# GLA stage of a hybrid encoder: keys, inner tiles and v in split float32r, gated outputs transposed from float32r copies

## The chip, the cores and the metric

The kernel runs on one core of one Trainium2 chip. The metric is the device time of one execution in microseconds. The profile is one execution on the chip, recorded by the hardware profiler; PE is the matrix engine, PEld its weight loads, DVE the vector engine, ACT the scalar engine, POOL the GpSimd engine and SP the engine whose queue issues most loads. A queue's name ends in q (ACTq, SPq).

## What is computed

The reference is an encoder of two layers over 512 tokens of width 1024, all in float32. Layer 0 mixes tokens with bidirectional gated linear attention (GLA), layer 1 with softmax attention, and each is followed by a gated MLP with a width-3 convolution. Only the GLA mixer of layer 0 is touched. It has 4 heads with 128 key and 256 value columns each:

```python
def gla_chunked(q, k, v, log_a, strict):          # per head; one call forward, one on flipped inputs
    b = jnp.cumsum(log_a, axis=3)                  # within chunks of 64 tokens
    q_dec, k_inv = q * jnp.exp(b), k * jnp.exp(-b)
    att = jnp.where(mask, q_dec @ k_inv.T, 0.0)    # inner products of a chunk
    o_intra = att @ v
    kv_chunk = (k * jnp.exp(b_end - b)).T @ v      # what a chunk adds to the state
    ...                                            # state[n+1] = decay_chunk * state[n] + kv_chunk
    o_inter = q_dec @ s_prev
    return o_intra + o_inter

o = o_f + o_b
o = rmsnorm(o, norm_w) * jax.nn.silu(g)
return o @ w_out
```

## The kernel before

The kernel keeps the residual x as eight tiles of 128 features x 512 tokens (x[c]). Weights stream in over SP's queue into two raw buffers; the class Weights turns each half of 128x1024 into a high part in float32r (ACT copy, L220) and a low part (DVE subtract, L221). A product of two such split operands is three float32r matmuls: high x high, high x low, low x high (mm3, L385). A matmul on plain float32 tiles shows in the trace as two matmul records. L86 is the helper that issues nearly all matmuls, so they are told apart by the tile that they write.

Instructions are traced in the order of the program, and a scheduler at compile time then fixes each engine's queue: by the written order as priority, with what is ready by its own timing going first. So an engine's order can differ from the written one, but on the chip each engine follows its fixed queue. Tiles come from pools by tag with a number of buffers each: in SBUF "g" (22 buffers of 128x1024), "xhl" (8), and in the stage "t" (6) and "u" (4) of 128x512; in PSUM "acc" (3 banks), "s" (2), "pt" (2) and "po" (1).

The GLA stage, function gla (L462):

- Four segments (seg, L474) project the normalised input to v and g, in token layout: 4 PSUM banks per segment, one for each block of 128 tokens, 512 columns (two heads) wide. seg_out (L481) evicts each bank with one DVE instruction that scales by the norm (L485). v and g are four tiles each, one per token block, holding all heads. Beside the segments run eight gates (gate, L532; two directions x 4 heads): a PE product z, then Abs, Exp and Ln on ACT, a POOL subtract (L544), a DVE scan, and two Exp that make EK (L563, L564).
- proj(h) (L581) makes k and q of head h, 24 float32r matmuls each. After proj(0), SiLU of g runs on ACT (L688) and POOL multiplies by the norm weights (L689), tile by tile.
- The loop over heads (L691) writes proj(h+1) and then core(h). core first multiplies EK by k and q (DVE, L597, L598) and makes "end" on POOL (L601). Then come the key transposes kt (three per direction, L608) and their copy to kts (ACT, L610); the inner products in (4 token blocks x 2 directions, float32, L620), put together in the tile at by an ACT copy (L622) and a predicated DVE copy (L625); per direction three products kv of kts and v (float32, L643) and their state updates (ACT L644, DVE L646). The third product of each direction goes to the one "po" bank. Then comes tail(h-1). Last, the outputs o (L667): per token block at with v, and EK with the states of one or both directions, all float32; then squares on ACT (L671), the inverse root (DVE L319, POOL L321) and the gating into g (DVE, L674).
- tail(h) (L676) transposes the two 128-column chunks of head h's gated output on PE (float32, L680) and splits them into oT (ACT L682, DVE L683), which lies in buffers of tag "xhl"; these come free as proj(3) finishes with the normalised input.
- The output projection op (out_steps, L426) runs twelve steps (chunks 0 to 5 for two pairs of output tiles), then tail(3), then the rest.

Of the kernel before, what the change touches and what calls it, by code (L numbers as in the profile page):

```python
# [59 lines left out]
def hybrid_encoder_kernel(  # L60
# [47 lines left out]
    def big(dt, n):  # L108
        return pair("g", 22, dt, n)
# [352 lines left out]
    def gla(norm, nxt):  # L462
# [5 lines left out]
        gc = big(F32, "gconst")  # L468
        mfull = gc[:, 0 : S + 1]
        gnw = gc[:, 640 : 640 + DV]  # L470
        v = [big(F32, "v") for _ in range(NT)]
        g = [big(F32, "g") for _ in range(NT)]

        def seg(i, between=None):  # L474
            ps = [bank(tag, "vg") for tag in SEG_BANKS[i]]
# [4 lines left out]

        def seg_out(ps, dst, h):  # L481
            for j in range(NT):
                o = dst[j][:, h * S : (h + 1) * S]
                r = norm.rtok[:, j : j + 1]
                dve.tensor_scalar(o, ps[j], r, None, ALU.mult)  # L485


        ps = seg(0)
# [100 lines left out]
            dve.scalar_tensor_tensor(kqt[:, :S], psq, DK ** -0.5, norm.R, ALU.mult, ALU.mult)  # L589
            return kqt  # L590

        def core(h, kqt, then):
            ends = big(F32, "end")
            ends = [ends[:, :S], ends[:, S:]]
            for d in range(2):
                e, f = EK[h, d], ends[d]
                dve.tensor_tensor(e[:, S:], e[:, S:], kqt[:, S:], ALU.mult)  # L597
                dve.tensor_tensor(e[:, :S], e[:, :S], kqt[:, :S], ALU.mult)  # L598
# [5 lines left out]
            orders, keys = ([0, 1, 2], [3, 2, 1]), []  # L604
            for d, order in enumerate(orders):
                kt = bank("pt", "kt")
                for i, s in enumerate(order):
                    pe.transpose(kt[:, i * P : (i + 1) * P], ends[d][:, s * P : (s + 1) * P], ident)  # L608
# [4 lines left out]
            at = tmp("t", "at")  # L613
            banks = []
            for d in range(2):
                e = EK[h, d]
                b = bank("acc" if h == GH - 1 else "s", "in")
# [6 lines left out]
            def upper():  # L624
                dve.copy_predicated(at3, msk, banks[1].rearrange("p (s c) -> p s c", c=P))  # L625

            at3 = at.rearrange("p (s c) -> p s c", c=P)
            msk = smask.rearrange("p (o c) -> p o c", o=1).to_broadcast([P, NT, P])

            st = {}  # L630
            hs = slice(h * DV, (h + 1) * DV)
            for d, order in enumerate(orders):
                kts = keys[d]
                sa = tmp("t", "sa")
                sb = tmp("t", "sb") if d == 0 else st["b"]
                st["b"] = sb
                step = 1 if d == 0 else -1
                kv = bank("acc", "kv")
                kv2 = bank("po", "kv2")
                place = [kv[:, :DV], kv[:, DV:], kv2[:, :DV]]  # L640
                slot = [sa[:, :DV], sa[:, DV:], sb[:, d * DV : (d + 1) * DV]]
                for i, s in enumerate(order):
                    mm(place[i], kts[:, i * P : (i + 1) * P], v[s][:, hs], start=True, stop=True)  # L643
                act.activation(slot[0], place[0], AF.Copy)  # L644
                for i in (1, 2):
                    last = dve.scalar_tensor_tensor(slot[i], slot[i - 1], FK[h, d][:, order[i] : order[i] + 1],  # L646
                                                    place[i], ALU.mult, ALU.add)
                for i, s in enumerate(order):
                    st[d, s + step] = slot[i]
                if d == 0:  # L650
                    with tc.issue_after(last.ins) if h == GH - 1 else ExitStack():
                        upper()
            if then is not None:
                then()

            oss = tiny(4, "oss")
            og = []
            for s in range(NT):
                if s % 2 == 0:
# [3 lines left out]
                for d in range(2):  # L663
                    if (d, s) in st:
                        parts.append((EK[h, d][:, s * P : (s + 1) * P], st[d, s]))
                for i, (l, r) in enumerate(parts):
                    mm(po, l, r, start=i == 0, stop=i == len(parts) - 1)  # L667
                og.append(po)
            for s in range(NT):
                junk = tmp("sq", "junk", DV)  # L670
                act.activation(junk, og[s], AF.Square, accum_out=oss[:, s : s + 1])  # L671
            ors = rsqrt_eps(oss, NT, "ors", 1.0 / DV)
            for s in range(NT):
                dve.scalar_tensor_tensor(g[s][:, hs], og[s], ors[:, s : s + 1], g[s][:, hs], ALU.mult, ALU.mult)  # L674

        def tail(h):  # L676
            for c in (2 * h, 2 * h + 1):
                tp = bank("pt", "tp")
                for s in range(NT):
                    pe.transpose(tp[:, s * P : (s + 1) * P], g[s][:, c * P : (c + 1) * P], ident)  # L680
                t = pair("xhl", 8, F32R, "oT")
                act.activation(t[:, :S], tp, AF.Copy)  # L682
                dve.tensor_tensor(t[:, S:], tp, t[:, :S].bitcast(F32), ALU.subtract)  # L683
                oh[c] = (t[:, :S], t[:, S:])

        kqt = proj(0)
        for j in range(NT):
            act.activation(g[j], g[j], AF.Silu)  # L688
            pool.tensor_tensor(g[j].rearrange("p (h c) -> p h c", c=DV), g[j].rearrange("p (h c) -> p h c", c=DV),  # L689
                               gnw.rearrange("p (o c) -> p o c", o=1).to_broadcast([P, GH, DV]), ALU.mult)  # L690
# [545 lines left out]
```

## Time and profile before

| what | value |
|---|---|
| median of 3 runs | 1117.07 us (1115.98 to 1118.34) |
| the profiled execution's own time | 1119.08 us |
| its span, first to last instruction | 1117.4 us |
| mean granted TensorE clock | 0.998 |
| GLA stage: segments and gates | about 5 to 104 us |
| GLA stage: heads, from k(0) to the end of o(3) | about 104 to 188 us |
| output projection | about 188 to 233 us |

The MLP of layer 0 follows until about 600 us, attention until about 745, the MLP of layer 1 to the end. In a row of a timeline stand the start in us, the duration, the engine, the line, the operation, out<-in with their tiles, the shape and a count; in brackets the idle time of the engine before it and what ended that. The chain of waits has the start, the duration and what the chain ran over. Matmul durations in the timeline overlap, since matmuls are pipelined; the chain's steps do not overlap, so that its duration over its count is the time one matmul takes from the next.

### The profile page before, as it was taken

Reading aid. Unit: us, or ns where it says so; the run is one execution under the profiler, and the core shown is the slowest. Engines: PE = TensorE matmul, PEld = TensorE weight load, DVE = VectorE, ACT = ScalarE, POOL = GpSimd, SP = SyncE. Lnnn points to the kernel's source line nnn. Section 1 sums busy time; section 2 is a strip of 40 time slices with the busy share of each in tenths; the row PEclk is TensorE's granted clock in tenths of the full one; section 3 lists DMA queues with packets and bytes.
Section 4 is the critical chain, followed back from the end, with each engine's and each line's share of the span. In section 5 each row is a group of like instructions: output and inputs, shape, how many; then the busy total and the mean of one; then the engine's idle time right before and its main releaser. Section 6 shows DMA issues by size and latency. Waiting matters only on the chain.

```text
span 1117.4 us, 16142 instructions
## 1 busy us (share of the span) xinstructions
PE 1104.9 (99%) x6418; PEld 974.1 (87%) x6418; DVE 864.3 (77%) x1325; ACT 601.0 (54%) x892; POOL 105.9 (9%) x96
## 2 busy tenths in 40 slices
PE   9999999999999999999999999999999999999998
PEld 7878888888899999999978887788879999999997
DVE  6566655459989999979885567654998999997985
ACT  6455224367645455544464788845764545544541
POOL 0213310021000000000004332101100000000000
PEclk9999999999999999999999999999999999999999
DMA  6323211368332322323337754446863232332322
GB/s 219 128 78 111 76 40 37 113 140 198 135 113 95 113 92 98 115 74 114 136 76 200 180 164 117 152 127 145 191 173 114 96 113 81 109 114 76 114 76 76
DMA packets 30938, 131.78 MB, mean 118 GB/s; under 512 B 3600, under 2 KB 4240, under 8 KB 22160
## 3 DMA queue, kind: packets, MB, share of 16 engines
q1 hardware_dynamic: 20496, 102.30, 27.5%
q0 software_dynamic: 5472, 19.93, 9.2%
q10 hardware_dynamic: 4896, 8.54, 2.1%
q8 instruction: 50, 0.82, 0.3%
q14 instruction: 24, 0.20, 0.1%
HBM read 100.34 MB, written 2.10 MB: 92 GB/s over the span
## 4 chain that ended last, share of the span: by engine, by line
PE 91%; DMA 3%; DVE 3%; ACT 2%; issue 1%; POOL 0%; SPq 0%; DVEq 0%; POOLq 0%; ACTq 0%
PE dn L86 20%; PE Y L86 16%; PE X L86 12%; PE up L86 9%; PE op L86 8%; PE vg L86 5%; PE A L86 3%; PE B L86 2%; PE po L86 2%; PE k L86 2%; PE q L86 2%; PE s L86 2%; DMA wl<-raw 2%; PE o L86 2%; PE av L86 1%
## 5 line engine op out<-in xcount | busy, mean ns | idle before, releaser
L86 PE MATMUL dn<-gu,wh 128*128 128x512 f32 x708 | 218.5, 390 | 0.8 <-DVE x L842 0.7
L86 PEld LDWEIGHTS dn<-gu,wh 128*128 128x128 f32 x708 | 130.4, 188 | 26.8 <-DVE x L842 2.1
L86 PE MATMUL dn<-gu,wl 128*128 128x512 f32 x354 | 137.4, 388 | 0.0
L86 PE MATMUL up<-xhl,wh 128*128 128x512 f32 x384 | 118.7, 390 | 0.0
L776 ACT ACTIVATE y<-u,cw 128x512 f32<-128x512 f32 x88 | 67.9, 808 | 78.4 <-DVE u L876 64.2
L167 ACT ACTIVATE wh<-raw 128x1024 fp32r<-128x1024 f32 x72 | 76.2, 1058 | 60.7 <-DVE raw L199 15.3
L86 PE MATMUL X<-th,xwh 128*128 128x256 f32 x360 | 101.9, 283 | 0.0
L86 PE MATMUL X<-th,xwl 128*128 128x256 f32 x360 | 101.9, 283 | 0.0
L86 PE MATMUL X<-tl,xwh 128*128 128x256 f32 x360 | 101.9, 283 | 0.0
L842 DVE TENSOR_TENSOR x<-x,dn 128x512 f32<-128x512 f32 x95 | 64.7, 684 | 27.9 <-PE dn L86 27.7
L167 ACT ACTIVATE wh<-draw 128x1024 fp32r<-128x1024 f32 x44 | 46.7, 1061 | 70.5 <-PE dn L86 35.5
L86 PEld LDWEIGHTS up<-xhl,wh 128*128 128x128 f32 x384 | 71.8, 188 | 14.7
L86 PE MATMUL vg<-wh,xhl 128*128 128x512 f32 x256 | 81.9, 398 | 1.4 <-DVE g L485 0.5
L210 POOL DMA_DIRECT2D wl<-raw x38 | 33.4, 878 | 515.0 <-ACT wl L169 508.7
L86 PEld LDWEIGHTS dn<-gu,wl 128*128 128x128 f32 x354 | 66.5, 188 | 13.8
L86 PE MATMUL up<-xhl,wl 128*128 128x512 f32 x192 | 75.0, 391 | 0.9 <-DMA wl<-raw 0.8
L86 PE MATMUL Y<-th,wh 128*128 128x256 f32 x264 | 74.7, 283 | 0.0
L86 PE MATMUL Y<-tl,wh 128*128 128x256 f32 x264 | 74.7, 283 | 0.0
L86 PE MATMUL Y<-th,wl 128*128 128x256 f32 x264 | 74.7, 283 | 0.0
L86 PE MATMUL op<-oT,wh 128*128 128x512 f32 x256 | 72.2, 395 | 0.0
L86 PEld LDWEIGHTS X<-th,xwh 128*128 128x128 f32 x360 | 69.0, 192 | 0.8 <-DVE v L856 0.7
L86 PEld LDWEIGHTS X<-tl,xwh 128*128 128x128 f32 x360 | 69.1, 192 | 0.1
(232 smaller groups left out, 2810.9 us busy)
## 6 DMA issues: line engine op xcount, KB each, us to landing
raw<-in_w_up_dram SPq DMA_DIRECT2D x44, 1024.0 KB, 5.0
draw<-in_w_down_dram SPq DMA_DIRECT2D x44, 512.0 KB, 3.8
wl<-raw POOLq DMA_DIRECT2D x38, 512.0 KB, 5.8
pr<-p ACTq DMA_DIRECT2D x32, 256.0 KB, 2.9
raw<-in_w_vg_dram SPq DMA_DIRECT2D x6, 1024.0 KB, 5.0
raw<-in_w_akq_dram SPq DMA_DIRECT2D x5, 1024.0 KB, 6.6
raw<-in_w_kq_dram SPq DMA_DIRECT2D x4, 1024.0 KB, 4.9
raw<-in_w_gout_dram SPq DMA_DIRECT2D x4, 1024.0 KB, 4.9
```

Of the source, the lines that this page charges most:

```text
L86: i = pe.matmul(*a, **k)
L167: act.activation(hi, r, AF.Copy)
L210: pool.dma_start(dst, src, accum_op=ALU.add)
L776: act.activation(yt, ut, AF.Identity, scale=w(1), bias=w(3))
L842: dve.tensor_tensor(x[c], x[c], ps, ALU.add)
```

## The change

- v and g become four tiles each by head, a tile holding all four token blocks of a head. seg_out evicts each bank with two DVE instructions of 256 columns.
- A helper split makes a float32r high part (ACT copy) and a low part (DVE subtract). It is applied to v of the head (vh, vl, 128x1024), to the transposed keys (kth, ktl, 128x384 for each direction) and to the inner tile after the predicated copy (ath, atl, 128x512).
- kv is then three float32r matmuls per product, and so is the product of the inner tile with v in o. The products of EK with the states, and in, stay float32.
- core is cut in three: scaled(h) (the multiplications by k and q, "end" and the split of v), inner(h) (kt, its split, in, and the ACT copy of at) and core (kv, states, at's predicated copy and split, o, gating). scaled(0) is written ahead of SiLU and proj(1). For the next head, scaled(h+1) is written between tail(h-1) and o(h); for head 3 inner(3) as well. inner of heads 0 to 2 stays behind proj(h+1).
- After the gating a DMA on ACT's queue copies g[h] (512 KB) into a float32r tile "gr", and tail transposes from that with a float32r identity.
- The PSUM tags of in stay as they were ("s" for heads 0 to 2, "acc" for head 3); at moves from tag "t" to "u". SiLU and the norm weights now go head by head.

```diff
+EARLY_INNER = (3,)
+IN_BANKS = ("s", "s", "s", "acc")
+AFTER = (False, False, False, True)
+AT_TAG = "u"
...
-                o = dst[j][:, h * S : (h + 1) * S]
                 r = norm.rtok[:, j : j + 1]
-                dve.tensor_scalar(o, ps[j], r, None, ALU.mult)
+                for e in range(2):
+                    dve.tensor_scalar(dst[2 * h + e][:, j * DV : (j + 1) * DV], ps[j][:, e * DV : (e + 1) * DV], r, None,
+                                      ALU.mult)
...
+        def split(y, hi, lo):
+            act.activation(hi, y, AF.Copy)
+            dve.tensor_tensor(lo, y, hi.bitcast(F32), ALU.subtract)
+
+        def scaled(h, kqt):
...
+            vh, vl = big(F32R, "vh"), big(F32R, "vl")
+            split(v[h], vh, vl)
+            return ends, vh, vl
...
+        def inner(h, ends):
...
-                kts = tmp("t", "kts")
-                act.activation(kts[:, : 3 * P], kt[:, : 3 * P], AF.Copy)
-                keys.append(kts)
+                kh, kl = tmp("t", "kth", 3 * P, F32R), tmp("u", "ktl", 3 * P, F32R)
+                split(kt[:, : 3 * P], kh, kl)
+                keys.append((kh, kl))
...
-                    mm(place[i], kts[:, i * P : (i + 1) * P], v[s][:, hs], start=True, stop=True)
+                    ks, vs = slice(i * P, (i + 1) * P), slice(s * DV, (s + 1) * DV)
+                    mm3(place[i], kh[:, ks], kl[:, ks], vh[:, vs], vl[:, vs], True, True)
...
-                    with tc.issue_after(last.ins) if h == GH - 1 else ExitStack():
-                        upper()
-            if then is not None:
-                then()
+                    with tc.issue_after(last.ins) if AFTER[h] else ExitStack():
+                        dve.copy_predicated(at.rearrange("p (s c) -> p s c", c=P), msk,
+                                            upper.rearrange("p (s c) -> p s c", c=P))
+                        ah, al = tmp(AT_TAG, "ath", dt=F32R), tmp("t", "atl", dt=F32R)
+                        split(at, ah, al)
+            nxt_ready = then()
...
-                parts = [(at[:, s * P : (s + 1) * P], v[s][:, hs])]
...
+                mm3(po, ah[:, ks], al[:, ks], vh[:, vs], vl[:, vs], True, False)
+                parts = [(EK[h, d][:, ks], st[d, s]) for d in range(2) if (d, s) in st]
...
+            gated[h] = big(F32R, "gr")
+            act.dma_start(gated[h].bitcast(F32), g[h])
+            return nxt_ready
...
-                    pe.transpose(tp[:, s * P : (s + 1) * P], g[s][:, c * P : (c + 1) * P], ident)
+                    at_ = s * DV + c % 2 * P
+                    pe.transpose(tp[:, s * P : (s + 1) * P].bitcast(F32R), gated[h][:, at_ : at_ + P], identr)
...
+        def ready(h, kqt, early):
+            ends, vh, vl = scaled(h, kqt)
+            return [inner(h, ends) if early else ends, vh, vl]
+
+        now = ready(0, proj(0), False)
+        for j in range(GH):
             act.activation(g[j], g[j], AF.Silu)
...
         for h in range(GH):
-            nxtk = proj(h + 1) if h + 1 < GH else None
-            core(h, kqt, (lambda: tail(h - 1)) if h else None)
-            kqt = nxtk
+            kqt = proj(h + 1) if h + 1 < GH else None
+            if h not in EARLY_INNER:
+                now[0] = inner(h, now[0])
+
+            def between():
+                if h:
+                    tail(h - 1)
+                return ready(h + 1, kqt, h + 1 in EARLY_INNER) if h + 1 < GH else None
+
+            now = core(h, now, between)
```

More of the change, by code (lines that the diff above doesn't have):

```diff
@@ L470, in gla @@
         gnw = gc[:, 640 : 640 + DV]
-        v = [big(F32, "v") for _ in range(NT)]
-        g = [big(F32, "g") for _ in range(NT)]
+        v = [big(F32, "v") for _ in range(GH)]
+        g = [big(F32, "g") for _ in range(GH)]
         def seg(i, between=None):
@@ L590, in proj @@
             return kqt
-        def core(h, kqt, then):
+        def split(y, hi, lo):
+            act.activation(hi, y, AF.Copy)
+            dve.tensor_tensor(lo, y, hi.bitcast(F32), ALU.subtract)
+        def scaled(h, kqt):
             ends = big(F32, "end")
@@ L602, in core @@
                                    .to_broadcast([P, 3, P]), ALU.mult)
-            orders, keys = ([0, 1, 2], [3, 2, 1]), []
+            vh, vl = big(F32R, "vh"), big(F32R, "vl")
+            split(v[h], vh, vl)
+            return ends, vh, vl
+        orders = ([0, 1, 2], [3, 2, 1])
+        msk = smask.rearrange("p (o c) -> p o c", o=1).to_broadcast([P, NT, P])
+        def inner(h, ends):
+            keys = []
             for d, order in enumerate(orders):
@@ L616, in core @@
                 e = EK[h, d]
-                b = bank("acc" if h == GH - 1 else "s", "in")
+                b = bank(IN_BANKS[h], "in")
                 for s in range(NT):
@@ L622, in core @@
             act.activation(at, banks[0], AF.Copy)
[L624 to L628, printed above, removed]
+            return keys, at, banks[1]
+        def core(h, ready, then):
+            (keys, at, upper), vh, vl = ready
             st = {}
-            hs = slice(h * DV, (h + 1) * DV)
             for d, order in enumerate(orders):
-                kts = keys[d]
+                kh, kl = keys[d]
                 sa = tmp("t", "sa")
@@ L684, in tail @@
                 oh[c] = (t[:, :S], t[:, S:])
-        kqt = proj(0)
-        for j in range(NT):
+        gated = {}
+        def ready(h, kqt, early):
[3 more added lines that the diff above has]
+        for j in range(GH):
             act.activation(g[j], g[j], AF.Silu)
```

11 lines of the change are left out of this document (5 added, 6 removed).

## Prediction

> **What bounds the kernel now.** I read the page first: the head and the engine line, then the sections on DMA issues. PE is busy for 99% of the span.
>
> ```profile
> span 1117.4 us, 16142 instructions
> PE 1104.9 (99%) x6418; PEld 974.1 (87%) x6418; DVE 864.3 (77%) x1325; ACT 601.0 (54%) x892; POOL 105.9 (9%) x96
> ...
> draw<-in_w_down_dram SPq DMA_DIRECT2D x44, 512.0 KB, 3.8
> ...
> pr<-p ACTq DMA_DIRECT2D x32, 256.0 KB, 2.9
> ```
>
> An average over stages does not say what this stage is worth, so I cut the GLA stage out with the view by stretches: first the v/g segments and the first projections, then the four heads up to the output projection. The columns are the stretch and its length, then busy time (and instructions) of PE, of its weight loads, of DVE, ACT and POOL, the granted clock, the DMA share and GB/s.
>
> ```profile
> 0.00:126.00 126.00, 123.29 (x536) 101.35 (x537) 83.36 (x125) 65.60 (x99) 29.46 (x24) 1.00 0.39 131
> 126.00:210.00 84.00, 83.97 (x433) 71.62 (x432) 40.83 (x72) 27.33 (x68) 9.77 (x10) 1.00 0.13 45
> ```
>
> In 126 to 210 us, where the products that change lie, PE has 0.03 us free of 84 at full granted clock (1.00), DVE 43 us free, ACT 57. So matmul time taken out here shortens the run, as long as the operands come in time. The chain of waits, cut to head 1, gives the price of each matmul: nearly every step is PE following PE.
>
> ```profile
> 146.17 0.66 PE kt L608 x6
> 146.82 1.79 PE in L86 x16
> 148.61 2.16 PE kv L86 x10
> 150.77 0.33 PE tp L680 x3
> 151.10 0.65 PE kv L86 x2
> 151.75 0.55 PE tp L680 x5
> 152.29 4.32 PE o L86 x20
> ```
>
> A float32 product is recorded as two matmuls: kv has 6 products and 12 records per head, at 0.216 each, so 0.432 us a product of 256 columns. A float32 transpose is one record, 0.11 us.
>
> **The change part by part.** *Matmuls.* The same chain, at later places of this kernel, has both replacements: 256-column products in split float32r (the FFN's X) and transposes from a float32r copy (attention's pt).
>
> ```profile
> 311.53 1.44 PE X L86 x12
> ...
> 672.99 0.30 PE pt L1087 x4
> ```
>
> A float32r record of 256 columns takes 0.12, three of them 0.36: 0.072 less than 0.432. 24 kv products (6 x 4 heads) and 16 products of the inner tile with v (4 x 4) make 40 x 0.072 = 2.9 us. A float32r transpose takes 0.075 against 0.11, and 32 of them (8 x 4) save 1.1 us. The kt transposes, the in products and the state products of o stay float32. PE gain: 4.0 us, all on the path.
>
> *Splits.* Each head gains on DVE one 128x1024 subtract (vl), two 128x384 (ktl) and one 128x512 (al), on ACT the copies vh and ah, and a DMA issue. DVE's own order in head 1 was:
>
> ```profile
> 146.21 0.69 DVE L589 SCALAR_TENSOR_TENSOR kq<-q,R 128x512 f32<-128x512 f32 x1 [2.29 <-PE q L86]
> 146.93 0.69 DVE L598 TENSOR_TENSOR ek<-ek,kq 128x512 f32<-128x512 f32 x1
> 147.54 1.22 DVE L221 TENSOR_TENSOR wl<-raw,wh 128x1024 fp32r<-128x1024 f32 x1
> 148.68 0.69 DVE L598 TENSOR_TENSOR ek<-ek,kq 128x512 f32<-128x512 f32 x1
> 149.28 0.72 DVE L625 COPY_PREDICATED at<-smask,in 128x512 f32<-128x512 uint8 x1
> 149.93 0.48 DVE L646 SCALAR_TENSOR_TENSOR sa<-sa,fk,kv 128x256 f32<-128x256 f32 x1
> 150.51 0.48 DVE L646 SCALAR_TENSOR_TENSOR sb<-sa,fk,kv 128x256 f32<-128x256 f32 x1
> ...
> 158.87 1.66 DVE L674 SCALAR_TENSOR_TENSOR g<-o,ors,g 128x256 f32<-128x256 f32 x4 [1.12 <-POOL ors L321]
> ...
> 163.48 1.33 DVE L683 TENSOR_TENSOR oT<-tp,oT 128x512 fp32r<-128x512 f32 x2
> ```
>
> vl costs 1.22 (the wl row), al 0.64 (second of the two oT: 1.33 - 0.69). A 128x384 subtract lies between 0.39 (four 256-wide in 1.66, so (1.66 - 0.48)/3 apart) and 0.64; I take 0.5. That is 1.22 + 1.0 + 0.64 = 2.9 a head, 11.5 in all: DVE goes from 40.8 to about 52 of 84 us. ACT gains a 128x1024 copy, a 128x512 copy and an issue. In busy time both are covered; the question is the order in one head.
>
> Head 1, from the end of q: PE did kt, in, kv and tp in 6.1 us (146.17 to 152.29). Now kv takes 6 x 0.36 = 2.16 and tp 8 x 0.075 = 0.6, so 0.66 + 1.79 + 2.16 + 0.6 = 5.2 us, and al is wanted 0.24 later (third matmul of its triple): 151.6. DVE stands at 149.28 after the row at 148.68; then come ktl twice (1.0), the predicated copy (0.65), two state updates (1.16) and al (0.64): 152.7, or 1.1 late. But the row at 148.68 belongs to the next head, and the weight split at 147.54 to a projection that starts after o: with both behind, al is ready at 151.0 and nothing waits. While PE waits, the other three at products hold only if al is there, and queued behind them are the state products, the gating and the next k. I take the middle, 0.5 us, for heads 0 and 1. Heads 2 and 3 have other PE work by the new order: inner(3) (kt and in, 2.4 us) stands between kv(2) and o(2), and the output projection's matmuls over chunks of earlier heads need nothing of head 3. Zero there, with 1.1 each as the upper end. Sum 1.0, bounds 0 and 4.4.
>
> *v and g by heads.* Each 512-wide eviction becomes two of 256. The four of g's first half, and the waits that ended with evictions:
>
> ```profile
> 82.61 2.72 DVE L485 TENSOR_SCALAR g<-vg,rtok 128x512 f32<-128x512 f32 x4
> ...
> 83.41 0.50 PE L86 MATMUL vg<-wh,xhl 128*128 128x512 f32 x1 [0.55 <-DVE g L485]
> ...
> PEld z L86 <- DVE gm L541: 0.5, 1, 0.5
> PE vg L86 <- DVE v L485: 0.3, 1, 0.3
> ```
>
> Four take 2.72, 0.66 apart; a pair of 256 takes 2 x 0.39 = 0.79. That is 0.13 more for each bank and 0.52 for four. PE waited for the first bank twice (v 0.3, g 0.55), so 0.26; and the z product waits for gm, which stands on DVE behind all four: up to 0.52, of which I take half, since DVE's order can be redrawn. Sum 0.5, bounds 0 and 0.8.
>
> *Gated outputs by DMA.* The copy is 512 KB; issue to landing lay at 2.9 us for 256 KB from this queue and 3.8 for 512 KB from another. Heads 0 and 1 have a whole projection before their tail (two of the 5.44 us steps quoted below), head 3 twelve output steps: hidden. Head 2 is a rival below. The issue on ACT's queue waits for the last gating; behind it stand the next head's weight copies, which wait for PE anyway.
>
> *Keys ahead.* scaled(h+1) moves in front of o(h): its POOL and DVE work had been done by then in large part (the row at 148.68). Nothing added.
>
> Sum: -4.0 + 1.0 + 0.5 = -2.5 us. The profiled execution took 1119.08 (1117.4 of span, 1.7 around it) and would take 1116.6; the median of the runs, 1117.07, lies 2.0 under it, and I apply the same difference: 1114.6. What a measurement of this kernel can tell from no change is about 0.2%, 2.2 us.
>
> *A rule against the change.* vl reads two SBUF tensors, as the weight splits do, and head 0's falls near POOL's products of g with the norm weights:
>
> ```profile
> 109.46 5.44 PE q L86 x24
> 114.90 5.44 PE k L86 x24
> ...
> 104.51 11.99 POOL L689 TENSOR_TENSOR g<-g,gconst 128x1024 f32<-128x1024 f32 x4 [8.42 <-ACT g L688]
> ...
> 110.83 3.42 DVE L221 TENSOR_TENSOR wl<-raw,wh 128x1024 fp32r<-128x1024 f32 x1
> ```
>
> Beside POOL such a subtract took 3.42 for 1.22, 2.2 more. It finished at 114.25, just before k(1) begins at 114.90. Another 1.22 on DVE there could therefore cost PE up to 1.2 + 2.2 - 0.65 = 2.8 us once. Against it: g of heads 0 and 1 is now whole after the third segment, so half of POOL's 12 us can be over earlier; I leave it in the range. The Trainium skill (SBUF — State Buffer, "SBUF: two separate sides") says that the pair of ports that DVE and GpSimd share is a lock held for a whole instruction; by that an instruction is blocked for up to one POOL product, 3.0 us here, and the sum would be -2.5 + 3.6 = +1.1. The row's 2.2 bears it out in kind.
>
> **The rivals.** *DVE gives the gain back (no change).* If PE keeps the written order, al is 1.1 late in each of four heads, and the evictions cost 0.8: -4.0 + 4.4 + 0.8 = +1.2, or 1118.3. For it: in the DVE rows above there is no gap from 146.21 on. Against: PE's queue does not follow the written order, as o begins before the last kv product in head 0.
>
> ```profile
> 130.22 0.59 PE L86 MATMUL o<-v,at 128*128 128x256 f32 x2
> 130.67 0.70 PE L86 MATMUL kv<-v,kts 128*128 128x256 f32 x2
> ```
>
> *SiLU goes in among the gates (no change).* g of heads 0 and 1 is complete near 86 us (82.61 + 2.72 + 0.5), before the last gate's Exp and Ln, and ACT has a gap there.
>
> ```profile
> 90.28 0.20 ACT L565 ACTIVATE fk<-fk 128x3 f32<-128x3 f32 x1 [4.62 <-DVE fk L559]
> ...
> 92.75 1.23 DVE L221 TENSOR_TENSOR wl<-raw,wh 128x1024 fp32r<-128x1024 f32 x1 [2.17 <-ACT wh L220]
> ...
> 101.26 1.28 ACT L688 ACT_TABLE_LOAD   x1
> 105.29 2.94 ACT L688 ACTIVATE g<-g 128x1024 f32<-128x1024 f32 x3
> ```
>
> Two more loads (1.28 each) and two SiLUs (1.0 each) make 4.6, just the gap of 4.62. A microsecond or two of excess delays wh and the split at 92.75, wanted about 94.5 by the fourth segment's third quarter (24 matmuls a quarter, so 83.41 + 2 x 5.44, and z), with 0.5 to spare: 0.5 to 2 us of PE, net -2.0 to -0.5, so 1115.1 to 1116.6. The Trainium skill (ScalarE: Activation LUTs, "What ACT_TABLE_LOAD costs") gives about 2.66 us a switch with its drain; two would then take 7.3 with the SiLUs and give about -0.3. No run here shows that drain.
>
> *Head 2's tail waits for its copy (slower).* One mechanism: with inner(3) moved ahead of o(2), only kv(3) (2.2 us) is written between o(2) and the transposes of head 2. Gating ended 3.9 us after o(2):
>
> ```profile
> 177.39 0.59 PE L86 MATMUL o<-sb,ek 128*128 128x256 f32 x2
> ...
> 180.24 1.66 DVE L674 SCALAR_TENSOR_TENSOR g<-o,ors,g 128x256 f32<-128x256 f32 x4 [1.12 <-POOL ors L321]
> ```
>
> That is 181.9 against 177.98, and the copy adds 2.9 to 3.8: about 7.4 in all, so PE stands for 7.4 - 2.2 = 5.2 us if tp(2) is queued before o(3) and the output projection. -2.5 + 5.2 = +2.7, or 1119.8. It decides from about 4.7 us of wait on. Against it is again the reordering seen at 130.22.
>
> That the change doesn't do what it says is hardly open: both float32r forms are in this trace at these shapes.
>
> **How the numbers follow.** Forecast (gain kept, small waits) 0.55; DVE gives it back 0.18; SiLU among the gates 0.12; tail waits 0.15. Faster 0.55, same 0.30, slower 0.15. The forecast's own range is 1113.0 (no waits) to 1114.9. With the two cases of no change and the runs' scatter (1115.98 to 1118.34) the range is 1112.7 to 1118.5; it leaves out the slower case.
>
> **What would show it.** In the changed profile: kv in 72 records at 0.12 apart, o with the inner tile in 48; tp at 0.075; 126 to 210 shorter by about 3 us with PE still above 98%. Right if PE's waits there are under 1.5 us. Wrong if a wait of PE on al, ktl or on the copy of g adds up to 3 us or more, if table loads stand between 80 and 100 us with a wait of vg on wl behind them, or if another stage moves by more than a microsecond.

## The result and the profile after

| | median | runs | ratio to the kernel before, 95% interval |
|---|---|---|---|
| kernel before | 1117.07 us | 7 (1115.98 to 1119.38) | |
| changed kernel | 1121.28 us | 7 (1119.85 to 1123.79) | 1.0035 (1.0022 to 1.0049) |

The change made the kernel slower by 0.35%, about 4 us. The forecast was 1114.6 and the range ended at 1118.5: sign and range were both wrong. (A few slow executions, of 1349 to 6242 us, count in the medians given here but are left out of the ratios, and the profile of one experiment, filler_in_the_wait, was such a one, at 1349 us and a granted clock of 0.75, and is not read.)

The head of the page after, first the span, then the busy time of each engine:

```profile
span 1118.1 us, 16272 instructions
## 1 busy us (share of the span) xinstructions
PE 1101.3 (98%) x6458; PEld 973.0 (87%) x6458; DVE 879.6 (79%) x1357; ACT 615.8 (55%) x907; POOL 108.4 (10%) x96
```

PE's busy time did fall, by 3.6 us (from 1104.9), and yet the run is longer: PE now stands still somewhere. The profiled execution took 1119.85 us. Its first segment was 2.1 us shorter (the first rp record at 28.6 and not 30.7 us), but that is the luck of a start: the profiles below have 28.3 to 31.1 there, kernels of both sorts at either end. So two spans cannot be subtracted. I measure from a landmark to a landmark instead: from the first kv record (the first product that changes) to the first up record (the first MLP).

| from the timelines | first kv | first up | distance |
|---|---|---|---|
| before | 128.06 | 233.07 | 105.01 |
| before, second profile (below) | 127.52 | 232.54 | 105.02 |
| changed | 125.99 | 233.38 | 107.39 |
| changed, second profile (below) | 126.25 | 232.48 | 106.23 |

The view by stretches shows where in it. It has the columns named in the prediction; before first, then after.

```profile
126.00:135.00 9.00, 9.00 (x53) 7.92 (x51) 5.43 (x9) 3.57 (x10) 0.00 (x0) 1.00 0.16 66
```

```profile
126.00:210.00 84.00, 80.75 (x454) 70.35 (x453) 51.74 (x87) 29.11 (x71) 9.76 (x9) 0.96 0.21 76
126.00:135.00 9.00, 5.78 (x26) 5.29 (x25) 8.32 (x13) 1.44 (x4) 0.77 (x1) 0.64 0.34 117
```

All 3.2 us that PE lacks in 126 to 210 us are missing in the first nine, in head 0, where DVE is full (8.32 of 9) and the granted clock is 0.64. PE's waits from 30 to 240 us and its timeline at that place name the rest:

```profile
PE kv L90 <- DVE ktl L599: 3.2, 1, 3.2
PE vg L90 <- DVE v L489: 1.3, 1, 1.3
PE vg L90 <- DVE g L489: 0.2, 1, 0.2
```

```profile
126.19 0.28 PE L90 MATMUL kv<-vl,kth 128*128 128x256 f32 x1
129.70 0.58 PE L90 MATMUL kv<-vh,ktl 128*128 128x256 f32 x1 [3.22 <-DVE ktl L599]
130.08 0.41 PE L90 MATMUL kv<-vh,kth 128*128 128x256 f32 x1
130.29 0.41 PE L90 MATMUL kv<-vl,kth 128*128 128x256 f32 x1
...
135.51 0.28 PE L90 MATMUL kv<-vh,kth 128*128 128x256 f32 x1
135.63 0.28 PE L90 MATMUL kv<-vl,kth 128*128 128x256 f32 x1
```

The third matmul of the first kv product waits 3.2 us for the low half of the keys. Behind the wait the records stand 0.21 us apart; from 135.5 on, they stand 0.12 apart. So the gap is paid twice, once as idle time and once as 5.8 us at nearly half pace. At 0.12 a record those 5.8 us would have been about 3.2, so the slow pace costs some 2.6 us more (an estimate from these rows). One head later the chain of waits shows what had been forecast:

```profile
151.80 1.79 PE kv L90 x15
153.59 0.63 PE tp L699 x8
154.22 0.54 PE o L90 x4
...
155.23 0.43 PE kv L90 x3
...
155.89 3.54 PE o L90 x20
```

That is 0.119 a kv record (1.79 for 15; three more follow in a row of their own) and 0.079 a transpose. The 24 records of o take 0.54 and 3.54, 4.08 us, where 20 float32 records took 4.32 before. In the chain, from the first q record of head 2 to up, 92.52 us (140.72 to 233.24) became 89.62 (143.92 to 233.54): the matmul gain is there, 2.9 us from head 1's key transposes to the end of the output projection.

Why ktl is late stands in the queues ahead of it. ACT from 82 us on:

```profile
82.55 1.28 ACT L713 ACT_TABLE_LOAD   x1
83.84 1.06 ACT L713 ACTIVATE g<-g 128x1024 f32<-128x1024 f32 x1
84.92 1.28 ACT L547 ACT_TABLE_LOAD   x1
86.22 0.63 ACT L547 ACTIVATE ga<-ga 128x512 f32<-128x512 f32 x1
...
87.82 1.28 ACT L548 ACT_TABLE_LOAD   x1
```

SiLU of head 0's g went in as soon as that tile was whole, in the middle of the gates. After a SiLU the gate's Exp (L547) and its Ln (L548) each load a set of their own. From 30 to 107 us there are eight loads, where the kernel before had one. The last gate ends late, and g of the fourth segment is evicted late. Before, then after:

```profile
102.60 2.72 DVE L485 TENSOR_SCALAR g<-vg,rtok 128x512 f32<-128x512 f32 x4
```

```profile
105.80 3.22 DVE L489 TENSOR_SCALAR g<-vg,rtok 128x256 f32<-128x256 f32 x8
...
110.79 5.00 DVE L606 TENSOR_TENSOR ek<-ek,kq 128x512 f32<-128x512 f32 x2
115.71 1.84 DVE L225 TENSOR_TENSOR wl<-raw,wh 128x1024 fp32r<-128x1024 f32 x1
117.48 1.84 DVE L599 TENSOR_TENSOR vl<-v,vh 128x1024 fp32r<-128x1024 f32 x1
...
126.00 1.84 DVE L599 TENSOR_TENSOR vl<-v,vh 128x1024 fp32r<-128x1024 f32 x1
127.77 0.68 DVE L594 SCALAR_TENSOR_TENSOR kq<-q,R 128x512 f32<-128x512 f32 x1
128.48 0.69 DVE L607 TENSOR_TENSOR ek<-ek,kq 128x512 f32<-128x512 f32 x1
129.09 1.02 DVE L599 TENSOR_TENSOR ktl<-kt,kth 128x384 fp32r<-128x384 f32 x2
```

Counted from the first rp record, the evictions began at 71.9 us and begin at 77.2 now, 5.3 later, and from there DVE has no gap. Three things can be read here: the evictions start late, two ek take 2.5 us each (0.69 elsewhere), and vl and ek of head 1 (126.00 to 129.1) stand ahead of head 0's ktl. Beside the slow ek, POOL does the last two products with the norm weights:

```profile
109.80 5.44 POOL L714 TENSOR_TENSOR g<-g,gconst 128x1024 f32<-128x1024 f32 x2 [8.03 <-ACT g L713]
```

### The profile page after: what moved, and what is told of

It reads as the page before. It is cut to its first block, busy times and chain, and to the rows that moved or that the text cites. A ratio compares the mean times of both kernels' runs of the same rounds, so it can differ in the third digit from the quotient of the medians.

```text
span 1118.1 us, 16272 instructions
## 1 busy us (share of the span) xinstructions
PE 1101.3 (98%) x6458; PEld 973.0 (87%) x6458; DVE 879.6 (79%) x1357; ACT 615.8 (55%) x907; POOL 108.4 (10%) x96
## 4 chain that ended last, share of the span: by engine, by line
PE 88%; DVE 5%; ACT 3%; issue 2%; DMA 1%; POOL 1%; SPq 0%; DVEq 0%; POOLq 0%; ACTq 0%
PE dn L90 20%; PE Y L90 16%; PE X L90 12%; PE up L90 10%; PE op L90 8%; PE vg L90 3%; PE A L90 2%; PE B L90 2%; PE po L90 2%; PE s L90 2%; PE o L90 1%; PE k L90 1%; PE av L90 1%; PE q L90 1%; DMA wl<-raw 1%
## 5 line engine op out<-in xcount | busy, mean ns | idle before, releaser
L808 ACT ACTIVATE y<-u,cw 128x512 f32<-128x512 f32 x88 | 67.8, 806 | 79.6 <-DVE u L908 64.1
```

The lines of the kernel that those rows point to most:

```text
L808: act.activation(yt, ut, AF.Identity, scale=w(1), bias=w(3))
```

## The experiments

Theory A: SiLU among the gates, with its table loads, makes the gates and all behind them late. Rival B: DVE's own new work (narrow evictions, vl of head 0 and 1) ahead of ktl does it, with or without A. The first four runs stand against one set of runs of the kernel before (1116.99), the next four against another (1116.75), then four (1118.02) and three (1116.99). The table at the end has all ratios.

**silu_behind_gates.** A alone is taken away.

```diff
+            exps[:] = [act.activation(e[:, :S], a, AF.Exp, scale=1.0 / 16),
...
+            with tc.issue_after(exps[0].ins), tc.issue_after(exps[1].ins), tc.issue_after(exps[2].ins):
                 act.activation(g[j], g[j], AF.Silu)
```

> The changed kernel with SiLU of g held behind the last gate's Exp on ACT; everything else, and PE's order, as changed. Theory A (SiLU by heads slips in between the gates, makes 8 table loads of 1.28 us out of 1, and the backlog on ACT and DVE reaches head 0's ktl): 1 table load before 126 us, g of the fourth segment evicted near 103 again instead of 105.8, PE's wait on ktl in head 0 under 1.5 us instead of 3.4, granted clock 1.00 there, total about 5 us under the changed kernel, 1 to 2 us under the kernel before (ratio to before 0.998). Theory B (the backlog is DVE's own new work, vl of heads 0 and 1 and the narrow evictions, ahead of ktl): the wait on ktl stays above 2 us and the total stays within 1.5 us of the changed kernel (ratio to before 1.002 to 1.004).

1116.98 us, ratio 1.0004 (0.9991 to 1.0016): the loss against before is gone. One table load is left where there were eight:

```profile
L714 ACT ACT_TABLE_LOAD x1 | 1.3, 1283 | 0.0
```

PE's wait on ktl, however, only shrinks from 3.2 to 1.9, between what A (under 1.5) and B (over 2) had said, so A is a part and B another. The evictions of the fourth segment come earlier by the same 1.3 us, 75.9 us behind the first rp record, and not by 5.3: SiLU of heads 0 and 1 now stands behind the gates but still ahead of a weight copy on ACT, for which DVE is idle 3.04 us just before them. The pace behind the wait is worth a look: it was full at first and halved 1.2 us later.

```profile
128.74 0.39 PE L90 MATMUL kv<-vh,ktl 128*128 128x256 f32 x1 [1.91 <-DVE ktl L599]
128.96 0.28 PE L90 MATMUL kv<-vh,kth 128*128 128x256 f32 x1
129.08 0.28 PE L90 MATMUL kv<-vl,kth 128*128 128x256 f32 x1
...
130.31 0.42 PE L90 MATMUL kv<-vl,kth 128*128 128x256 f32 x1
130.52 0.42 PE L90 MATMUL kv<-vh,ktl 128*128 128x256 f32 x1
```

**by_heads_alone.** The kernel before with v and g by heads, everything in float32: A with the narrow evictions, without splits.

```diff
-                o = dst[j][:, h * S : (h + 1) * S]
...
+                for e in range(2):
+                    dve.tensor_scalar(dst[2 * h + e][:, j * DV : (j + 1) * DV], ...)
```

> The kernel before with only v and g held by heads (two 256-wide evictions for one of 512, SiLU and norm weights head by head); all products float32, no DMA copy, no keys ahead. Theory A: the extra table loads appear here too; the gates' chain ends about 3 us later, and without the added splits head 0 still absorbs part: +0.5 to +3 us to before (ratio 1.0005 to 1.0027). Theory B: evictions cost 0.5 us, no more: ratio 0.999 to 1.001, and DVE on time at head 0.

1117.99 us, ratio 1.0013 (1.0000 to 1.0025), first kv to first up 105.31. The table loads are all there, and PE has one wait of 0.3 us from the first kv on, on sb: late gates alone cost little where no ktl is wanted early. A needs B.

**scaled_after_outputs.** Head h+1's scaling and vl are written behind the outputs of head h, for heads 1 and 2.

```diff
-                return ready(h + 1, kqt, h + 1 in EARLY_INNER) if h + 1 < GH else None
+                return ready(h + 1, kqt, True) if h + 1 in EARLY_INNER else None
...
+            if now is None and h + 1 < GH:
+                now = ready(h + 1, kqt, False)
```

> The changed kernel with scaled(h+1) written behind o(h) for heads 0 and 1 (the next head's multiplications and v split no longer ahead; head 3 as changed), so that vl of head 1 (1.84 us) stands behind ktl of head 0 on DVE. Theory A: the table loads stay (8), the wait on ktl shrinks by vl's 1.8 us to about 1.6, the clock is not throttled, total 3 to 4 us under the changed kernel (ratio to before 1.000). Theory B: wait gone, total 5 to 6 us under the changed kernel (ratio 0.998).

1117.57 us, ratio 1.0009 (0.9997 to 1.0020). The table loads stay, the wait on ktl falls from 3.2 to 0.8 us, and the records behind it are 0.12 apart. In the trace only vl and POOL's "end" of head 1 have moved; ek of head 1 still stand ahead of head 0's ktl. What went is vl(1), 1.84 us, and the 0.6 us that a weight split there had lost beside "end" (1.85, now 1.22): the larger part of the wait.

**filler_in_the_wait, filler_again.** 24 more products of kth and vh on head 0's first place, overwritten by the right ones, fill the gap without shortening it.

```diff
+                if h == 0 and d == 0:
+                    for _ in range(24):
+                        mm(place[0], kh[:, :P], vh[:, :DV], start=True, stop=True)
```

> The changed kernel with 24 matmuls more on PE in head 0 (kth and vh, in float32r, to the bank of the first kv product, which then overwrites them), so that PE works through most of its wait for ktl (24 x 0.12 = 2.9 of 3.4 us). If half of the loss is the clock that PE loses by idling (granted 0.64 in 126 to 135 us), the clock stays 1.00, kv goes at 0.12 a record again, and the total falls by 2 to 3 us below the changed kernel (ratio to before 1.001). If the wait alone is the loss, nothing changes (ratio 1.0035, same clock dip). Under both theories A and B the time at which ktl is ready stays.

> filler_in_the_wait once more, for its trace: the changed kernel with 24 extra products of kth and vh on head 0's first place, overwritten by the right ones, which fill PE's wait on ktl. If the half clock follows from the idle time: the granted clock from 126 to 135 us goes from 0.64 to 0.95 or more, records after the wait are 0.12 us apart and not 0.215, and 2 to 3 us of the loss go though no wait on ktl is shortened. If the clock drops at that place for another reason: 0.64 stays, and the time is that of the changed kernel, 1120 to 1122.

1118.78 us, 1.0020 (1.0007 to 1.0032), and 1119.28 us, 1.0018 (1.0008 to 1.0029): more work, and 0.08 to 0.17% less time than the changed kernel (1.0035 and, repeated, 1.0028), with intervals that overlap. The granted clock in these nine microseconds is 1.00:

```profile
126.00:135.00 9.00, 8.12 (x67) 7.62 (x64) 8.96 (x11) 3.40 (x7) 2.92 (x2) 1.00 0.36 117
```

So here the idle time brought the slow clock. The trace shows less of the gain than expected: first kv to first up is 106.66, 0.7 under the changed kernel's first profile and 0.4 over its second, since waits of 0.3 on ktl, 0.6 on ath and 0.5 on sb follow; PE at full pace catches up with DVE again. My 2 to 3 us were too much.

**both_held_back, both_held_back_again.** silu_behind_gates and scaled_after_outputs together.

> The changed kernel with both edits that each took a part of the loss away: SiLU of g held behind the last gate's exponentials, and the next head's scaled keys and split v (heads 1 and 2) written after the outputs of the head before. Theory AB (the loss is the seven extra table loads plus DVE's new work ahead of head 0's ktl, and the half clock after the wait): one table load before 126 us, PE's wait on ktl under 0.5 us, granted clock near 1.00 from 126 to 135 us, the stretch from rp to the first up product under 200.3 us (the shorter of the two single edits), the whole 2 to 3 us under the kernel before, 1114 to 1115 us. Rival C (the two remedies take away the same thing, so that they do not add up): 1116.5 to 1117.5, like either alone. Rival D (the loss is the inner order of heads 1 to 3 with its waits on ath and atl): the wait on ath of 0.6 us and others grow, no gain.

> both_held_back once more. It gained 3.4 us between the first kv and the first up (101.62 where the kernel before has 105.01 and 105.02) and took 70.8 us and not 67.8 in the second FFN's up stage, 3.0 us longer. Theory O (that stage belongs to the kernel): 70.8 again, and 1116 to 1117. Rival L (luck of a profile): a distance nearer to 68, and with it a time under 1115.

No wait on ktl is left; from 30 to 240 us PE waits for evictions alone:

```profile
PE vg L90 <- DVE v L489: 1.3, 1, 1.3
PE vg L90 <- DVE g L489: 0.2, 1, 0.2
```

First kv to first up takes 101.62 us, both times: 3.4 us less than before, and less than with either edit alone (105.15 and 102.91), so rival C fell. Against the changed kernel's two profiles it is 5.8 and 4.6 us less. That is what their gap and slow pace come to: 3.2 and 2.6 us in the first, 3.2 and, with 2.9 us of slow pace, about 1.3 in the second. The whole gained less: 1116.34 us, 0.9991 (0.9977 to 1.0005), then 1115.78 us, 0.9984 (0.9971 to 0.9996). This is the version to keep: 0.44% under the changed kernel in both pairs of runs. Against the kernel before, the first set shows no clear difference and the second a gain of 0.16%.

**norm_product_left_out.** silu_behind_gates without POOL's products of g with the norm weights (left out of the computation): is DVE late by its count, or by POOL beside it?

```diff
-            pool.tensor_tensor(g[j].rearrange("p (h c) -> p h c", c=DV), ...
```

> The kernel with SiLU behind the gates, without GpSimd's products of g with the norm weights (that part of the computation is left out). What is open: whether DVE is late at head 0's ktl because its own new operations stand ahead of it, or because these operations are slow beside POOL's products (ek 2.50 each and vl 1.84 where others take 0.7 and 1.2). If POOL slows them: ek near 0.7 to 1.4 each, vl near 1.2, DVE gains some 4 us before ktl, PE's wait on ktl goes from 2.1 to 0, the clock stays near 1.00 from 126 to 135 us, time about 3 to 4 us under silu_behind_gates, 1113 to 1114.5. If it is DVE's own count: durations as they are, the wait stays near 2, time 1116.5 to 1117.5.

POOL it is. The two ek, at the same place, and then ktl:

```profile
111.00 1.29 DVE L606 TENSOR_TENSOR ek<-ek,kq 128x512 f32<-128x512 f32 x2
...
127.12 1.01 DVE L599 TENSOR_TENSOR ktl<-kt,kth 128x384 fp32r<-128x384 f32 x2
```

1.29 us for the two and not 5.00, 3.7 us back on DVE, and no wait on ktl: 101.70 us to up. POOL's products are not new, though. In the kernel before they slowed DVE as much at this place: beside the wl of 3.42 that the prediction shows stand

```profile
105.42 2.60 DVE L221 TENSOR_TENSOR wl<-raw,wh 128x1024 fp32r<-128x1024 f32 x1
114.17 2.89 DVE L597 TENSOR_TENSOR ek<-ek,kq 128x512 f32<-128x512 f32 x1
```

which makes 5.8 us over the 1.22, 1.22 and 0.69 of such operations elsewhere. There DVE still had idle stretches of 1.48 and 2.00 us between 105 and 126 us; with late evictions and vl it has none, and the same slowing reaches PE. The time, 1116.42 (0.9994, 0.9985 to 1.0004), is 2 us over what I expected, for a reason that lies behind the first MLP (below). vl took 1.84 here too: POOL's two products for end, 2.98 us, lie beside it.

**products_one_head_at_a_time.** both_held_back with POOL's products moved behind the outputs of the head before.

```diff
+        weigh(0)
...
+            if h + 1 < GH:
+                weigh(h + 1)
```

> both_held_back with GpSimd's products with the norm weights spread out: head 0's ahead as before, the one of each other head after the outputs of the head before it. norm_product_left_out showed what is to be had from it: ek at 0.69 us each in head 0 and not 2.50, no gap on PE from 100 to 189 us. Theory (POOL's products slow DVE only where they lie beside it): ek of head 0 near 0.7 to 1.4 us each, PE without a wait in GLA, the stretch from rp to up near that of norm_product_left_out, 0 to 1 us under both_held_back; the whole 1115 to 1116.5. Rival: the products now meet head 1's and 2's ek and g, and the time is taken there, 1116.5 to 1118.

A miss, and no test of the theory: the products moved in the program but not in POOL's queue. All four still run before 116.1 us, two of them beside the two ek of head 0, which take 5.00 us as before.

```profile
110.66 5.44 POOL L717 TENSOR_TENSOR g<-g,gconst 128x1024 f32<-128x1024 f32 x2 [1.65 <-ACT g L714]
```

101.63 us to up, as without the move; 1116.79 us, 0.9989 (0.9976 to 1.0002).

**float32r_transposes_alone, copy_behind_the_keys.** The kernel before by heads, plus the copy to gr and the float32r transposes; in the second, the copy of head h is issued behind the key copies of head h+1.

```diff
+            act.dma_start(gated[h].bitcast(F32), g[h])
...
-                    pe.transpose(tp[:, s * P : (s + 1) * P], g[h][...], ident)
+                    pe.transpose(tp[:, s * P : (s + 1) * P].bitcast(F32R), gated[h][:, at_ : at_ + P], identr)
```

> The kernel before with v and g by heads and the gated outputs copied to a float32r tile from ScalarE's queue and transposed from there; inner products, keys and v stay float32. By the sum of the prediction: 32 transposes by 0.035 us, 1.1 us less than by_heads_alone (1117.99), so about 1116.9, with the copy hidden in heads 0 to 2 and in head 3. By the rival (the tail of head 3 waits for its copy of 2.9 us): a wait of PE on gr of 1 to 3 us in front of the last eight transposes, and no gain or a loss, 1118 to 1120.

> float32r_transposes_alone with one move: on ScalarE's queue the copy of head h's gated outputs is issued behind the key copies of head h+1 and not ahead of them. What float32r_transposes_alone showed: the issue of head 2's copy waits on ScalarE for DVE's g, the key copies of head 3 stand behind it, PE waits 1.3, 0.2 and 0.7 us for them and then runs ten kv records in 3.98 us and not 2.16. Theory Q (a wait in ScalarE's queue ahead of the keys costs these 3 to 4 us): the waits of PE on kts and on end at 177 to 181 us go, the kv records take 2.2 us, time 2 to 3 us under float32r_transposes_alone, about 1117 to 1118. Rival T (the float32r transposes or the copy's traffic cost it): the waits stay or come back at tp, 1119.5 to 1120.5.

Alone, this part costs 2 us over by_heads_alone: 1120.08 us, 1.0031 (1.0021 to 1.0041). PE at head 3, then ACT and POOL at the same place:

```profile
179.11 0.55 PE L610 MATMUL kt<-ident,end 128*128 128x128 f32 x3 [1.33 <-POOL end L603]
179.90 0.55 PE L610 MATMUL kt<-ident,end 128*128 128x128 f32 x3 [0.24 <-POOL end L603]
181.11 1.22 PE L86 MATMUL kv<-v,kts 128*128 128x256 f32 x2 [0.66 <-ACT kts L612]
```

```profile
180.04 0.47 ACTq L679 DMA_DIRECT2D gr<-g  x1
180.56 0.87 ACT L612 ACTIVATE kts<-kt 128x384 f32<-128x384 f32 x2 [3.59 <-PE kt L610]
```

```profile
177.26 1.01 POOL L321 TENSOR_TENSOR ors<-ors,halfneg 128x4 f32<-128x4 f32 x1 [18.73 <-DVE ors L319]
178.23 1.61 POOL L603 TENSOR_TENSOR end<-ek,fk 128x384 f32<-128x384 f32 x2
```

Head 2's outputs have come ahead of head 3's keys in the queues. POOL had been idle for 18.73 us, waiting for head 2's sum of squares, with both end products of head 3 behind it; that is 1.6 of PE's 2.2 us. ScalarE's issue, which waits for the gating, held the first key copy by less than a microsecond. Behind these gaps ten kv records took 3.98 us and not 2.16. With the issue written behind the keys the compile-time order turns back, POOL does an end of head 3 at 165.48, and the waits on end and kts are gone: 1118.20 us, 0.9996 (0.9986 to 1.0006), 0.35% less. Theory Q is right that a queue does it and, by the waits, wrong on which: it was mainly POOL's. (The edit turned the order of both queues, so no run parts them.) The sum's 1.1 us do not show against by_heads_alone even then, 105.52 us to up and 105.31, with a wait of 0.9 us on sa. In the changed kernel inner(3) is written ahead of these outputs, and no such wait is there.

**sixteen_products_less, before_again, both_held_back_sixteen_less, changed_again.** What was open: the second MLP.

```diff
+                    if src is w_gout and k in (1, 2) and i == 1:
+                        continue
```

> The kernel before with 16 of the products of GLA's output projection left out (that part of the computation is missing), 16 by 0.227 us, 3.6 us of PE. What is open: both_held_back and norm_product_left_out reach the first FFN about 3 us earlier than the kernel before, and are timed at most 0.8 us faster; in their second FFN PE waits 2.2 us on a transfer of low weights (0.8 in the kernel before) and 46 products behind it take 12.3 us and not 10.7. If a gain ahead of the FFNs is given back there whatever its source: the time falls by 0 to 1.5 us, with a wait of 2 us or more on that transfer. If it is not: the time falls by 3 to 4 us, to 1113 to 1114, and the loss behind is the changed kernel's own.

> The kernel before, unchanged, for a second profile. If PE's wait on the low weights in the second FFN belongs to the kernel: 0.8 us again, and 67.8 us from the first product of up to the first of dn there. If it varies from run to run: another wait between 0 and 2.5 us, and a distance between 67 and 71.

> both_held_back with the 16 products of GLA's output projection left out as in sixteen_products_less (that part of the computation is missing): everything behind starts 3.6 us earlier. sixteen_products_less took 68.0 us in the second FFN's up stage, about what the kernel before takes. If the longer stage of both_held_back hangs on the moment at which it starts: a distance near 68 and a whole 5 us or more under both_held_back. If it hangs on the kernel and not on the moment: 70 to 71 again, and 3 to 4 us under both_held_back.

> The changed kernel once more, for a second profile and an interval of its own. If the stage behind belongs to the kernel (theory O): 69.2 us from the first product of up to the first of dn in the second FFN, where the kernel before has 67.8 twice, with a wait on low weights of 1.8 us; the first kv to the first up 107.4 us; the whole 1120.5 to 1121.5. If that stage goes by luck (rival L): another distance, 67 to 71, and a time that moves with it.

Leaving out 16 products on the kernel before gives 0.9955 (0.9940 to 0.9971), 3 to 7 us for 3.6 of PE: a gain ahead of the MLPs is not given back as such. before_again repeats its first profile (105.02 and 67.8). But where keys and v are split, the chain in the second MLP ends otherwise. Before, then both_held_back, the transfer of low weights and the products behind it:

```profile
811.60 9.37 DMA wl<-raw
...
821.00 10.74 PE up L86 x46
```

```profile
808.34 10.81 DMA wl<-raw
...
819.20 12.34 PE up L90 x46
```

The transfer takes 1.4 us longer, PE waits 2.2 and not 0.8 for it, and in some profiles the pace falls behind that wait: 12.34 us for 46 products, 10.74 at full pace. In both_held_back_again the wait was 1.4 and the pace full. The transfer took 10.4 to 11.3 us in all nine profiles of kernels with keys and v split and nothing left out of the output projection, and the pace fell in five of them; kernels without these splits, by heads or not, have 9.3 to 9.6 (by_heads_alone 9.54, issued 1.6 us later in the stage). So the slower transfer goes with the splits, and whether it halves the pace is luck of an execution. Why it is slower I could not find: it is issued at the same moment of the stage, 47.6 us after its first product, in both. With the 16 products left out, both_held_back_sixteen_less has 9.62 us again, 68.54 up to dn, and a time about 6 us under both_held_back: the branch in which the stage hangs on the moment at which it starts. But the moment alone does not decide it, since up begins at 763.95 in the kernel before and at 763.59 in the changed one, with 9.37 and 10.70. The cause stays open. The changed kernel's account is then +2.4 and +1.2 us up to the MLPs and +1.4 and +2.9 there, 3.8 and 4.1 in its two profiles, beside 4.2 and 3.7 by the clock (1.0035; 1120.70 us, 1.0028, 1.0017 to 1.0039).

| kernel | ratio | first kv to up | wait on ktl | second MLP, up to dn |
|---|---|---|---|---|
| before, before_again | 1, 0.9992 | 105.01, 105.02 | - | 67.80, 67.77 |
| changed, changed_again | 1.0035, 1.0028 | 107.39, 106.23 | 3.2, 3.2 | 69.17, 70.66 |
| silu_behind_gates | 1.0004 | 105.15 | 1.9 | 69.20 |
| by_heads_alone | 1.0013 | 105.31 | - | 69.57 |
| scaled_after_outputs | 1.0009 | 102.91 | 0.8 | 71.02 |
| filler_again | 1.0018 | 106.66 | 0.3 | 69.72 |
| both_held_back, again | 0.9991, 0.9984 | 101.62, 101.62 | 0 | 70.82, 68.83 |
| norm_product_left_out | 0.9994 | 101.70 | 0 | 70.89 |
| products_one_head_at_a_time | 0.9989 | 101.63 | 0 | 71.03 |
| float32r_transposes_alone | 1.0031 | 108.59 | - | 67.16 |
| copy_behind_the_keys | 0.9996 | 105.52 | - | 68.84 |
| sixteen_products_less | 0.9955 | 101.39 | - | 68.00 |
| both_held_back_sixteen_less | 0.9934 | 98.75 | 0 | 68.54 |

## Why the prediction was wrong

- **Matmuls, -4.0.** Right, if a little large. PE's busy time fell by 3.6 us, and with the waits in the heads taken away the stretch is 3.4 shorter.
- **Splits, the wait of 0.5 us in head 0.** This step failed. It took DVE's order in head 1, with ek at 0.69 and without any vl in it, for head 0 too. Head 0 has another order: the late evictions of g, ek beside POOL, two vl, and no slack. The wait was 3.2 us on ktl, over the 3 us that the prediction itself had named as a sign of being wrong (in no other head was there any; I had charged head 1 with 0.5 too). Taking away its causes one by one gave 3.2 to 1.9 (SiLU behind the gates), 3.2 to 0.8 (vl of head 1 behind the outputs), and 1.9 to 0 (POOL's products).
- **"Keys ahead. Nothing added."** Wrong: scaled(1) had become longer by vl, 1.84 us, and vl went past ktl(0) in DVE's queue.
- **SiLU among the gates.** Held at 0.12, it happened, and 1.3 us of the wait went with it. Its mechanism was right and its size wrong: I counted two more loads, there were seven, since Exp and Ln stopped sharing a set once SiLU had been loaded between. And the price came elsewhere, not as a wait of vg on a weight split but as late evictions on DVE. Each load took 1.28 us, and the next instruction followed at once (82.55 + 1.28, 83.84). The drain that the Trainium skill (ScalarE: Activation LUTs, "What ACT_TABLE_LOAD costs") adds to a switch does not show in these rows.
- **A rule against the change.** Bounded at +2.8 from a wl row beside POOL, kept in the range and left out of the sum. It was the right place and the wrong victim: ek, 2.50 each where 0.65 is the price without POOL; and the slowing was not new, only the room for it had gone. The Trainium skill (SBUF — State Buffer, "SBUF: two separate sides") has DVE and GpSimd shut each other out for a whole instruction. One product takes 2.72 us and one ek lost 1.85, so the trace agrees in kind.
- **No term for the clock.** A gap was priced at its length. Here it brought 3 to 6 us at nearly half pace (2.9 in changed_again, 5.8 in the first profile), a loss of about 1.3 and 2.6 us.
- **Evictions, +0.5.** The eight took 3.22 us for 2.72, as worked out, but from the first rp record to the first kv record both kernels take 97.4 us: nothing. **The copy** took 2.9 us for 512 KB and was hidden; **head 2's tail** waited for nothing, because the queue has o(3) and op ahead of it.
- **Nothing was said of the second MLP**, where the longer transfer and the pace behind it took 1.4 to 2.9 us of the loss; why it is longer stays open. So the step that failed in the heads accounts for the other 2.4 to 1.2 us of the loss, and for the 3.4 us of gain that did not come.

## What to carry to other kernels

When work is put in front of a stage, read the queue of each engine in the first head or tile, not in a typical one: what runs once (gates, evictions, norm weights) meets it there. Price a gap on PE with the slow records that may follow, and ask of every function that becomes ready earlier (here SiLU) whose table it throws out. An instruction that waits, on POOL or as a DMA issue on ACT, holds all that stands behind it in its queue.

## What the runs showed of the chip

- PE's pace fell after gaps of 1.9 to 3.2 us, not after each, and not always at once. After 1.91 us (silu_behind_gates) the pace was full for 1.2 us and then halved for 3.5; after 2.21 us (both_held_back, second MLP) 46 products took 1.6 more, and after 2.72 (filler_again, second MLP) nothing was lost. Shorter gaps close together did it too: behind 1.33, 0.24 and 0.66 us in float32r_transposes_alone ten kv records took 3.98 us for 2.16. The Trainium skill (TensorE: Matmul & The Clock Gate, "Part 1: The HAM clock gate (the "warmup" mystery)") has the clock follow PE's activity in a free-running window of about 3.4 us. Slow stretches that last 2.9 to 5.8 us, and one that begins late, fit a window that does not start with the gap, though no run here shows the window; that a gap must be as long as a window does not fit the 1.91 us, and there the measurement decides.
- DVE operations with two SBUF operands slow down beside POOL: two ek took 5.00 us for 1.29, a subtract of 128x1024 1.84 for 1.22 beside POOL's "end" and up to 3.42 beside its products with the norm weights.
